# First chunk of the down product: operand sums by adding DMA transfers, half of the gated values stored negated

## The chip, the cores and the metric

The kernel runs on one core of a Trainium2 chip. PE is the matrix engine, PEld its weight loads, DVE the vector engine, ACT the scalar engine, POOL the GpSimd engine, SP the engine that only issues DMAs. Each engine carries out its instructions in order; they meet through semaphores. The metric is device time in microseconds (us), the median of several runs of one kernel.

## What is computed

One decoder block over 512 tokens of 2048 channels in float32: a combined input projection that feeds two token mixers, an output projection, and a gated MLP with a causal convolution of width 3 between its up projection and its activation. The change lies in the MLP:

```python
h = _rmsnorm(x, norm2_g[l])
up = jnp.einsum('bsd,df->bsf', h, ffn_w_up[l])          # 2048 -> 2 * 6144
up = _causal_dwconv(up, ffn_conv_w[l], ffn_conv_b[l])
gate, val = jnp.split(up, 2, axis=-1)
x = x + jnp.einsum('bsf,fd->bsd', jax.nn.gelu(gate) * val, ffn_w_down[l])
...
return _rmsnorm(x, final_g)
```

## The kernel before

**Seven products in place of eight.** Both MLP products treat every operand as 2 x 2 blocks of 256 columns and use seven block products on sums and differences of the blocks (a Winograd form of Strassen's scheme). Each operand therefore is a tile of seven slots: the blocks themselves (slots 4 to 6, and 7 for making sums) and sums of them (slots 0 to 3). Every operand is also split into a high part in a rounded format (ACT, L126) and the rest (DVE, L127), and each product is three matmuls over these halves; a pair of such tiles is what PE reads.

**Units.** The work runs in units of one weight operand each: 192 for the up product (24 blocks of eight, blocks alternating between gate and value columns), then the down product in three chunks of 8, 8 and 6 operands, four blocks for each. A unit is 42 matmuls of 256 columns (`product`, L852), seven products of six; their order is 1, 2, 6, 5, 3, 7, 4. Unit 184 begins the last up block, unit 192 the first down block. Products gather in eight PSUM banks, seven for a block and one to spare, so the second product of a block takes over a bank of the block before. The banks are read at a block's end: in the up product by `combine` (ACT copies product 1, L868; DVE L869 to L876), in the down product by L969 to L979.

**The stream.** `stream` lists the operands in the order in which they are wanted: weights (`Weights`) for each unit, and, in the units 187 to 197, the activations of the down product's first chunk (`Acts`, eight operands, numbered 0 to 7 here; after units 187, 188, 190, 191, 193, 194, 196 and 197). `prepare` walks it and puts, for item n, the load of n+1, the sums of n+1, the split of n and the load of n+2 into the program. Loads go to SP's queue into one of three buffers `q`. The weights of most units load their four blocks (512 KB, L637) and DVE makes the sums (L646 to L648). Those of units 0 to 7 and of the units around each chunk's start (184 to 199 for the first) load prepared sums from memory instead (512 KB, L639) and three blocks (384 KB, L640). A unit's preparation is written ahead of its own matmuls, and reaches two units ahead.

**Sums prepared in memory.** POOL's queue issues DMA transfers that copy and add into DRAM tiles `made`; `make` (L315 to L322) takes the next ones from a list, a share of it in every unit of the up product. A transfer that adds to a tile waits on POOL for the one before it on that tile, and the list lays the four stages of a tile apart.

**The gated values.** In an up block of value columns, DVE finishes the convolution (L916), multiplies by the gate (L919), and POOL issues the store of the 512 columns into the DRAM tile `ad` (L921), 256 KB, two blocks of 256. This and the other steps of a block's tail are put off by `later` into units 1, 2, 4 and 5 of the block that follows. For the down product, `Acts.load` brings an `ad` tile back (L665) and `Acts.sums` makes its sums with three DVE instructions (L671 to L673):

```python
nc.vector.tensor_tensor(q[:, 2:4], q[:, 7:8].broadcast_to([P, 2, 256]), q[:, 5:7], ALU.subtract)
nc.vector.tensor_tensor(q[:, 1], q[:, 6], q[:, 2], ALU.subtract)
nc.vector.tensor_tensor(q[:, 0], q[:, 4], q[:, 1], ALU.subtract)
```

Of the kernel before, what the change touches and what calls it, by code (L numbers as in the profile page):

```python
# [8 lines left out]
F32 = mybir.dt.float32  # L9
# [3 lines left out]
ALU = mybir.AluOpType  # L13

P = 128
# [31 lines left out]
CHUNKS = [range(0, 8), range(8, 16), range(16, 22)]  # L47
# [31 lines left out]
def hybrid_block(ctx: ExitStack, tc: tile.TileContext, x, xT, w_in, w_out, w_up, w_dn, w_m4, w_dl, wab, wsT, vec, bs, vgb, fg, out):  # L79
    nc = tc.nc  # L80
# [213 lines left out]
    made = {}  # L294
# [13 lines left out]
    to_make = []  # L308
# [3 lines left out]
                to_make += copies[n] if part == 0 else added[n][0] if part == 1 else [added[n][1][part - 2]]  # L312
    pace = const.tile([P, 1], F32, name="pace")

    def make(n, after=None):  # L315

        if after is not None:
            nc.gpsimd.tensor_copy(pace, after)
        for _ in range(min(n, len(to_make))):
            add, dst, src = to_make.pop(0)  # L320
            how = {"accum_op": ALU.add} if add else {}
            nc.gpsimd.dma_start(dst, src, max_dma_last_dim=8192, **how)  # L322

# [192 lines left out]
    for i in range(2):  # L516
        for st in range(NS):
            t = vv[i][:, st]
# [5 lines left out]
    for i in range(2):  # L524
        ps = project(w_in, B_U + i, xg, True)
        t = rp.tile([P, 4, S], F32, name="uu", tag="r")
# [77 lines left out]
    ss2 = const.tile([P, NS, 4], F32, name="ss2")  # L604
    x2d = [tc.dram_tile([P, NS, 512], F32, name=f"x2d{d}") for d in range(4)]
    ad = [tc.dram_tile([P, 4, 256], F32, name=f"ad{i}") for i in range(NP)]

    def squares2(d):
        nc.gpsimd.dma_start(x2d[d], x2[d])
# [18 lines left out]
    class Weights:  # L628


        def __init__(self, src, made=None):
            self.src, self.made = src, made
# [9 lines left out]
        def sums(self):  # L642
            q = self.q
            if self.made is not None:
                return
            nc.vector.tensor_tensor(q[:, 2:4], q[:, 5:7], q[:, 7:8].broadcast_to([P, 2, 256]), ALU.add)  # L646
            nc.vector.tensor_tensor(q[:, 1], q[:, 2], q[:, 6], ALU.add)  # L647
            nc.vector.tensor_tensor(q[:, 0], q[:, 1], q[:, 4], ALU.add)  # L648
# [7 lines left out]
    class Acts:  # L656


        def __init__(self, m, src=None, fill=None):
            self.m, self.src, self.fill = m, src, fill  # L660

        def load(self):
            self.q = slots("q")
            if self.fill is None:
                nc.sync.dma_start(self.q[:, 4:8], self.src)  # L665
            else:
                self.fill(self.q)

        def sums(self):
            q = self.q  # L670
            nc.vector.tensor_tensor(q[:, 2:4], q[:, 7:8].broadcast_to([P, 2, 256]), q[:, 5:7], ALU.subtract)  # L671
            nc.vector.tensor_tensor(q[:, 1], q[:, 6], q[:, 2], ALU.subtract)
            nc.vector.tensor_tensor(q[:, 0], q[:, 4], q[:, 1], ALU.subtract)  # L673
# [33 lines left out]
    def rest_of_loads():  # L707
        while halves:
            halves.pop(0)()
# [54 lines left out]
    spread = (0, 1, 3, 4, 6, 7, 9, 10)  # L764
    after = {}
    for m in range(8):
        after.setdefault(max(2, m), []).append(Acts(m, fill=from_rows(m)))
    for c, s in zip(CHUNKS, starts):
        for i, p in enumerate(c):
            after.setdefault(s - 8 + spread[i] + 3, []).append(Acts(i, src=ad[p]))  # L770

    def half_tiles(d):
        if d < 3:
# [82 lines left out]
    def later(step, f):  # L856
        lazy.setdefault(step, []).append(f)
# [22 lines left out]
    def up_block(g, val, u0):  # L880
        q = {}
        for m in range(8):
            prepare(ready(u0 + m))
            for p in ORDER:
                product(q, p, act[m], stream[place[u0 + m]].hl, True, m == 0, m == 7)
                if p == 6:
                    rest_of_loads()
            make(len(to_make) - n_make + n_make * (u0 + m + 1) // (n_up - 16))
            if m == 7 and u0 == 0:
                pads[:] = [t_tile(f"pad{n}", [P, 2, S + 2]) for n in range(2)]  # L890
                for t in pads:
                    nc.gpsimd.memset(t[:, :, 0:2], 0.0)
            for f in lazy.pop(u0 + m, ()):
                f()
        c1 = t_tile("c1", [P, 2, 256])
        lo, hi = slice(2, 258), slice(258, 514)
        combine(q, c1, pads[0][:, :, lo], pads[1][:, :, lo], pads[0][:, :, hi], pads[1][:, :, hi])
        if u0 == 0:
            pools["ps"].release()
            pools["tr"].release()  # L900
            pools["ps"] = psum("q1", 8)

        def tap(n, j, f):
            if val:
                dst = t_tile("cv", [P, 2, S])if j == 0 else cvs[n]
                cvs[n] = dst
            else:
                if j == 0:
                    gates[n] = t_tile("gate", [P, 2, S], 2)
                dst = gates[n]  # L910
            nc.scalar.activation(dst[:, j], pads[n][:, j, 2:2 + S], AF.Identity, bias=col(V_FB + f), scale=col(V_FW + 2 * 96 + f))

        def rest(n, j, f):
            dst = (cvs if val else gates)[n][:, j]
            for i in (1, 0):
                nc.vector.scalar_tensor_tensor(dst, pads[n][:, j, i:i + S], col(V_FW + i * 96 + f), dst, ALU.mult, ALU.add)  # L916
            if val:
                gate = gates[n][:, j]
                nc.vector.tensor_tensor(gate, gate, dst, ALU.mult)  # L919
                at = 0 if j else 2  # L920
                nc.gpsimd.dma_start(ad[2 * g + n][:, at:at + 2], gate.rearrange("p (a b) -> p a b", a=2))  # L921

        def gelu(n, j):
            t = gates[n][:, j]
            nc.scalar.activation(t, t, AF.Gelu_apprx_tanh)

        cvs = {}
        at = u0 + 8
        for i, (n, j) in enumerate(((1, 0), (1, 1), (0, 0), (0, 1))):
            f = 48 * val + 4 * g + 2 * n + j  # L930
            step = at + (0, 1, 3, 4)[i]
            later(step, lambda n=n, j=j, f=f: tap(n, j, f))
            later(step + 1, lambda n=n, j=j, f=f: rest(n, j, f))
            if not val:
                later(step + 2, lambda n=n, j=j: gelu(n, j))

    pads = []
    for b, (g, val) in enumerate(ups):
# [6 lines left out]
    def down_block(ci, n, u0):  # L945
        tt = nc.vector.tensor_tensor
        size = len(CHUNKS[ci])
        q = {}
        for m in range(size):
            prepare(ready(u0 + m))  # L950
            if m == (6 if u0 == n_up else 1):
                if u0 == n_up:

                    pools["t"].release()
                    pools["x"] = pool("tx", "right")

            for half, at in ((0, 6 if u0 == n_up else 1), (1, 6 if u0 == n_up else 3)):
                if m == at:
                    t = pools["x"].tile([P, 2, 512], F32, name="xs", tag="xs", bufs=3)
                    nc.gpsimd.dma_start(t, x2d[n][:, 2 * half:2 * half + 2])  # L960
                    xs[n, half] = t
            for p in ORDER:
                product(q, p, act[m], stream[place[u0 + m]].hl, False, m == 0, m == size - 1)
            for f in lazy.pop(u0 + m, ()):
                f()
        X1, X2 = xs[n, 0], xs[n, 1]
        X11, X12, X21, X22 = X1[:, :, 0:256], X1[:, :, 256:512], X2[:, :, 0:256], X2[:, :, 256:512]
        c6, c5, c7 = (pools["x"].tile([P, 2, 256], F32, name="cc", tag="cc", bufs=3) for _ in range(3))
        tt(X11, X11, q[1], ALU.add)  # L969
        tt(X11, X11, q[2], ALU.add)  # L970
        nc.scalar.copy(c6, q[6])
        tt(c6, c6, q[1], ALU.subtract)
        nc.scalar.copy(c5, q[5])
        tt(X12, X12, q[3], ALU.add)
        nc.scalar.copy(c7, q[7])
        tt(X21, X21, q[4], ALU.add)
        steps = [
            lambda: tt(c5, c5, c6, ALU.add),
            lambda: tt(X12, X12, c5, ALU.add),  # L979
            lambda: tt(c6, c6, c7, ALU.add),  # L980
            lambda: tt(X21, X21, c6, ALU.subtract),
            lambda: tt(c5, c5, c7, ALU.add),
            lambda: tt(X22, X22, c5, ALU.add),
        ]
        if u0 + size == len(units):
            prepare(len(stream) - 2)
            for f in steps:
                f()
            prepare(len(stream) - 1)
            return  # L990
        at = u0 + size
        for i in range(3):
            later(at + i, steps[2 * i])
            later(at + i, steps[2 * i + 1])
        for half, t, step in ((0, X1, 0), (1, X2, 2)):
            later(at + step, lambda half=half, t=t: nc.gpsimd.dma_start(x2d[n][:, 2 * half:2 * half + 2], t))
# [6 lines left out]
    for n in DORD[:3]:  # L1003
        t = slots("q").rearrange("p a b -> p (a b)").rearrange("p (a b) -> p a b", a=NS)
# [9 lines left out]
    for st in range(NS):  # L1014
# [4 lines left out]
        for n, (i, d, lo, hi) in enumerate(pieces):  # L1019
# [6 lines left out]
            t = xs[d, st // 2][:, st % 2, lo:hi]  # L1026
# [10 lines left out]
        v, y, u, r = (const.tile([P, 1], F32, name=f"r3{c}", tag=f"r3{c}", bufs=2) for c in "vyur")  # L1037
# [7 lines left out]
        for n in order:  # L1045
            _, d, lo, hi = pieces[n]
# [74 lines left out]
```

## Time and profile before

| | |
|---|---|
| median of 3 runs | 2078.45 us (2078.12 to 2079.34) |
| the profiled execution | 2073.06 us, its span 2071.3 us |
| granted TensorE clock over the span | 0.995 |
| loads `q<-ad` of the down product's chunks | 22, 512 KB each, 3.1 to 7.8 us from issue to landing |
| transfers into `made` | 270 of 256 KB and 54 of 128 KB |
| stores `ad<-gate` | 48 of 256 KB |

Rows of a timeline give the start in us from the span's start, the duration, the engine, the line of the kernel, the operation, the tiles it writes and reads, and in brackets how long the engine sat idle before it and what released it. Rows of waits give who waited for whom, the total in us, how often, and the longest. Rows of groups give busy us, the mean of one in ns, and the idle time before. Rows of DMA issues give the queue that issued, how many, the size of each and the median us from issue to landing. Rows of stretches give the busy us of PE, PEld, DVE, ACT and POOL with their counts, the granted clock, the share of the 16 DMA engines' time, and GB/s. In names of tiles, `wh` and `wl` are the high and low halves of a weight, `ah` and `al` those of an activation, `qs` a PSUM bank, `q` a loaded operand.

### The profile page before, as it was taken

To read this page: it belongs to the slowest core of one execution; us is meant where nothing else is said; L and a number is where in the kernel's file an instruction comes from. 1 tells how busy PE (TensorE), PEld (TensorE's weight loads), DVE (VectorE), ACT (ScalarE), POOL (GpSimd) and SP (SyncE) were. 2 spreads that over 40 slices of the span, in tenths; PEclk is the share of its full clock that TensorE was granted. 3 is DMA by queue.
4 is the path that set the end of the run, shared out by engine and by line. 5 is a ranking of instruction groups with operands and counts; after the bars stand their busy time and mean duration, and the time that the engine had idled before them with its cause. 6 is when DMAs were issued, how large, how long until landed. Compare 5 with 4: busy or idle time off the path is not lost.

```text
span 2071.3 us, 35056 instructions
## 1 busy us (share of the span) xinstructions
PE 2037.6 (98%) x14528; PEld 1921.8 (93%) x14528; DVE 1732.0 (84%) x2183; ACT 906.6 (44%) x887; POOL 323.7 (16%) x510
## 2 busy tenths in 40 slices
PE   9999999999989999999999999999999999999998
PEld 8888888888789999999999999999999999999996
DVE  7598982745379999999999999999989979879986
ACT  6445322423274444444444444444455345345443
POOL 1332232211210202202202012022000000000001
PEclk9999999999999999999999999999999999999999
DMA  7666687656553746647557467466456568558564
GB/s 250 181 171 163 175 213 175 192 170 213 148 156 112 199 127 177 180 131 193 148 151 203 136 173 191 136 175 168 128 205 221 189 216 284 181 192 282 176 231 153
DMA packets 105904, 376.37 MB, mean 182 GB/s; under 512 B 14608, under 2 KB 22160, under 8 KB 91792
## 3 DMA queue, kind: packets, MB, share of 16 engines
q1 hardware_dynamic: 65808, 246.30, 35.1%
q0 software_dynamic: 39360, 127.17, 25.9%
q8 instruction: 113, 1.85, 0.4%
q10 hardware_dynamic: 576, 0.66, 0.1%
q14 instruction: 47, 0.39, 0.1%
HBM read 341.57 MB, written 110.36 MB: 218 GB/s over the span
## 4 chain that ended last, share of the span: by engine, by line
PE 76%; DVE 17%; DMA 4%; issue 2%; ACT 1%; DVEq 0%; SPq 0%; ACTq 0%
PE qs L852 46%; PE ps L162 9%; PE ps L164 9%; PE ps L163 9%; DVE wl L127 7%; DMA q<-w_up 3%; DVE q L646 2%; DVE al L127 1%; DVE q L647 1%; DVE cv L916 1%; DMA q<-w_dn 1%; PE qs L163 1%; PE qs L162 1%; PE qs L164 1%; DVE gate L916 1%
## 5 line engine op out<-in xcount | busy, mean ns | idle before, releaser
L852 PE MATMUL qs<-ah,wh 128*128 128x256 f32 x2688 | 765.1, 285 | 6.4 <-DVE pad L869 3.9
L852 PE MATMUL qs<-al,wh 128*128 128x256 f32 x2688 | 762.5, 284 | 0.0
L852 PE MATMUL qs<-ah,wl 128*128 128x256 f32 x2688 | 762.3, 284 | 0.0
L126 ACT CAST wh<-q 128x1792 fp32r<-128x1792 f32 (+1 forms) x282 | 476.8, 1691 | 597.5 <-PE qs L852 382.9
L127 DVE TENSOR_TENSOR wl<-q,wh 128x1792 fp32r<-128x1792 f32 (+1 forms) x282 | 567.7, 2013 | 43.6 <-ACT wh L126 43.3
L852 PEld LDWEIGHTS qs<-ah,wh 128*128 128x128 f32 x2688 | 517.3, 192 | 9.3 <-DVE pad L869 5.1
L852 PEld LDWEIGHTS qs<-al,wh 128*128 128x128 f32 x2688 | 517.3, 192 | 0.1
L852 PEld LDWEIGHTS qs<-ah,wl 128*128 128x128 f32 x2688 | 517.3, 192 | 0.0
L852 PE MATMUL qs<-wh,ah 128*128 128x256 f32 x1232 | 351.0, 285 | 7.0 <-ACT c L868 3.4
L852 PE MATMUL qs<-wl,ah 128*128 128x256 f32 x1232 | 350.2, 284 | 0.0
L852 PE MATMUL qs<-wh,al 128*128 128x256 f32 x1232 | 350.1, 284 | 0.0
L852 PEld LDWEIGHTS qs<-wh,ah 128*128 128x128 f32 x1232 | 237.8, 193 | 8.5 <-ACT c L868 3.6
L322 POOL DMA_DIRECT2D made<-w_m x324 | 234.9, 1061 | 54.0 <-DMA made<-w_m 44.8
L127 DVE TENSOR_TENSOR wl<-wraw,wh 128x1024 fp32r<-128x1024 f32 (+2 forms) x105 | 118.0, 1127 | 149.4 <-ACT wh L126 144.5
L852 PEld LDWEIGHTS qs<-wl,ah 128*128 128x128 f32 x1232 | 237.9, 193 | 0.2 <-DVE wl L127 0.2
L852 PEld LDWEIGHTS qs<-wh,al 128*128 128x128 f32 x1232 | 237.8, 193 | 0.0
L126 ACT CAST wh<-wraw 128x1024 fp32r<-128x1024 f32 (+2 forms) x105 | 102.1, 974 | 273.4 <-PE ps L163 146.4
L646 DVE TENSOR_TENSOR q<-q 128x512 f32<-128x512 f32 x226 | 154.8, 685 | 22.1 <-DMA q<-w_up 18.6
L921 POOL DMA_DIRECT2D ad<-gate x48 | 28.0, 583 | 828.3 <-DVE gate L919 828.3
L162 PE MATMUL ps<-xgh,wh 128*128 128x512 f32 x384 | 152.5, 398 | 0.0
L163 PE MATMUL ps<-xgl,wh 128*128 128x512 f32 x384 | 152.2, 397 | 0.0
L164 PE MATMUL ps<-xgh,wl 128*128 128x512 f32 x384 | 150.2, 396 | 0.0
(242 smaller groups left out, 2491.5 us busy)
## 6 DMA issues: line engine op xcount, KB each, us to landing
q<-w_up SPq DMA_DIRECT2D x176, 512.0 KB, 3.6
made<-w_m POOLq DMA_DIRECT2D x270, 256.0 KB, 5.9
wraw<-w_in SPq DMA_DIRECT2D x28, 1024.0 KB, 6.3
q<-made SPq DMA_DIRECT2D x54, 512.0 KB, 4.0
q<-w_dn SPq DMA_DIRECT2D x50, 512.0 KB, 3.8
wraw<-w_out SPq DMA_DIRECT2D x16, 1024.0 KB, 5.5
q<-w_dn SPq DMA_DIRECT2D x38, 384.0 KB, 4.6
ad<-gate POOLq DMA_DIRECT2D x48, 256.0 KB, 2.4
```

The source lines that it names most:

```text
L126: nc.scalar.copy(h, src)
L127: nc.vector.tensor_tensor(l, src, h.bitcast(F32), ALU.subtract)
L162: nc.tensor.matmul(ps, lhsT=ah, rhs=bh, start=start, stop=False)
L163: nc.tensor.matmul(ps, lhsT=ah, rhs=bl, start=False, stop=False)
L164: nc.tensor.matmul(ps, lhsT=al, rhs=bh, start=False, stop=stop)
L322: nc.gpsimd.dma_start(dst, src, max_dma_last_dim=8192, **how)
L646: nc.vector.tensor_tensor(q[:, 2:4], q[:, 5:7], q[:, 7:8].broadcast_to([P, 2, 256]), ALU.add)
L647: nc.vector.tensor_tensor(q[:, 1], q[:, 2], q[:, 6], ALU.add)
L852: nc.tensor.matmul(q[p][:, t], lhsT=x_, rhs=y_, start=first and t == 0 and n == 0, stop=last and t == 1 and n == 2, skip_group_check=True)
L916: nc.vector.scalar_tensor_tensor(dst, pads[n][:, j, i:i + S], col(V_FW + i * 96 + f), dst, ALU.mult, ALU.add)
L921: nc.gpsimd.dma_start(ad[2 * g + n][:, at:at + 2], gate.rearrange("p (a b) -> p a b", a=2))
```

## The change

For the eight operands of the first chunk, the sums are made in memory. Transfers on POOL's queue copy blocks of `ad` into a new DRAM tile `sums_of` and add further blocks to it, five transfers for each operand, one with every second unit from the 81st unit on. [...] `Acts.load` then brings the prepared sums (512 KB) and three blocks (384 KB), and `Acts.sums` does nothing for these operands. Where the down product's first chunk reads products that came out negated, additions become subtractions. The other two chunks stay as they were.

```diff
-    def make(n, after=None):
+    def make(n, after=None, todo=to_make):
...
-        for _ in range(min(n, len(to_make))):
-            add, dst, src = to_make.pop(0)
+        for _ in range(min(n, len(todo))):
+            add, dst, src = todo.pop(0)
...
+    sums_of = [tc.dram_tile([P, 4, 256], F32, name=f"as{i}") for i in CHUNKS[0]]
...
         def load(self):
             self.q = slots("q")
-            if self.fill is None:
+            if self.made is not None:
+                nc.sync.dma_start(self.q[:, 0:4], self.made)
+                nc.sync.dma_start(self.q[:, 4:7], self.src[:, 0:3])
+            elif self.fill is None:
                 nc.sync.dma_start(self.q[:, 4:8], self.src)
...
         def sums(self):
+            if self.made is not None:
+                return
...
+            if u0 >= 80 and m % 2:
+                make(1, todo=sum_up)
             make(len(to_make) - n_make + n_make * (u0 + m + 1) // (n_up - 16))
...
-                nc.vector.tensor_tensor(gate, gate, dst, ALU.mult)
+                if 2 * g + n in CHUNKS[0]:
+                    for t in (slice(0, 256), slice(256, 512)):
+                        nc.vector.scalar_tensor_tensor(gate[:, t], gate[:, t], -1.0 if (t.start == 0) == (j == 1) else 1.0, dst[:, t], ALU.mult, ALU.mult)
+                else:
+                    nc.vector.tensor_tensor(gate, gate, dst, ALU.mult)
...
+    sum_up = []
+    for k in range(len(CHUNKS[0]) + 3):
+        for r in range(4):
+            if 0 <= k - r < len(CHUNKS[0]):
+                dst, src = sums_of[k - r], ad[k - r]
+                sum_up += [
+                    [(0, dst[:, 0:2], src[:, 0:3:2]), (0, dst[:, 2:4], src[:, 1:3])],
+                    [(1, dst, src[:, 3:4].broadcast_to([P, 4, 256]))],
+                    [(1, dst[:, 0:2], src[:, 1:2].broadcast_to([P, 2, 256]))],
+                    [(1, dst[:, 0], src[:, 2])],
+                ][r]
...
+        plus = ALU.subtract if ci == 0 else ALU.add
...
-        tt(X11, X11, q[2], ALU.add)
+        tt(X11, X11, q[2], plus)
...
-        tt(X12, X12, q[3], ALU.add)
+        tt(X12, X12, q[3], plus)
...
-            lambda: tt(c5, c5, c6, ALU.add),
+            lambda: tt(c5, c6, c5, plus),
...
-            lambda: tt(c6, c6, c7, ALU.add),
+            lambda: tt(c6, c6, c7, plus),
...
-            lambda: tt(c5, c5, c7, ALU.add),
+            lambda: tt(c5, c5, c7, plus),
```

More of the change, by code (lines that the diff above doesn't have):

```diff
@@ L656, in hybrid_block, with __init__ @@
     class Acts:
-        def __init__(self, m, src=None, fill=None):
-            self.m, self.src, self.fill = m, src, fill
+        def __init__(self, m, src=None, fill=None, made=None):
+            self.m, self.src, self.fill, self.made = m, src, fill, made
         def load(self):
             self.q = slots("q")
-            if self.fill is None:
+            if self.made is not None:
+                nc.sync.dma_start(self.q[:, 0:4], self.made)
+                nc.sync.dma_start(self.q[:, 4:7], self.src[:, 0:3])
+            elif self.fill is None:
                 nc.sync.dma_start(self.q[:, 4:8], self.src)
@@ L769, in hybrid_block @@
         for i, p in enumerate(c):
-            after.setdefault(s - 8 + spread[i] + 3, []).append(Acts(i, src=ad[p]))
+            after.setdefault(s - 8 + spread[i] + 3, []).append(Acts(i, src=ad[p], made=sums_of[i] if c is CHUNKS[0] else None))
     def half_tiles(d):
```

## The prediction

> **What bounds the kernel now.** I read the page first, then the waits of PE, then three stretches of the trace. The page says that PE is busy nearly throughout, so only the places where it falls behind can be won:
>
> ```profile
> span 2071.3 us, 35056 instructions
> PE 2037.6 (98%) x14528; PEld 1921.8 (93%) x14528; DVE 1732.0 (84%) x2183; ACT 906.6 (44%) x887; POOL 323.7 (16%) x510
> ```
>
> The sums that the change takes off DVE stand at 1528 to 1594 us. In ten-microsecond stretches (busy time of PE, PEld, DVE, ACT, POOL; granted clock; DMA share) only two of that time are bad for PE, and the PE timeline shows the place, the first unit of the down product (unit 192):
>
> ```profile
> 1560.00:1570.00 10.00, 6.32 (x45) 5.82 (x44) 9.15 (x10) 6.13 (x6) 0.00 (x0) 0.85 0.69 243
> 1570.00:1580.00 10.00, 9.66 (x67) 9.66 (x68) 9.47 (x12) 3.98 (x4) 0.00 (x0) 0.80 0.41 143
> ...
> 1564.39 0.28 PE L852 MATMUL qs<-wh,al 128*128 128x256 f32 x1
> 1568.07 0.58 PE L852 MATMUL qs<-wh,ah 128*128 128x256 f32 x1 [3.40 <-ACT c L868]
> ...
> 1570.34 0.58 PE L852 MATMUL qs<-wh,ah 128*128 128x256 f32 x1 [0.62 <-DVE pad L869]
> ...
> 1574.05 0.28 PE L852 MATMUL qs<-wh,al 128*128 128x256 f32 x1
> 1574.17 0.28 PE L852 MATMUL qs<-wh,ah 128*128 128x256 f32 x1
> ```
>
> From 1564.39 to 1574.05 PE starts 24 matmuls (products 2, 6, 5 and 3 of the unit, six each). At the 0.12 us between the last two rows they need 2.9 us; they took 9.66. **This junction costs 6.8 us**: 3.4 and 0.6 of idle, the rest matmuls at a low clock. What was late, on ACT and DVE, with the load behind it on SP's queue:
>
> ```profile
> 1565.85 1.69 ACT L126 CAST ah<-q 128x1792 fp32r<-128x1792 f32 x1 [1.44 <-DVE q L673]
> 1567.44 0.58 ACT L868 COPY c<-qs 128x512 f32<-128x512 f32 x1
> ...
> 1560.10 0.32 SPq L665 DMA_DIRECT2D q<-ad  x1
> ...
> 1564.21 0.69 DVE L671 TENSOR_TENSOR q<-q 128x512 f32<-128x512 f32 x1 [0.75 <-DMA q<-ad]
> ...
> 1565.73 2.02 DVE L127 TENSOR_TENSOR wl<-q,wh 128x1792 fp32r<-128x1792 f32 x1
> 1567.67 2.02 DVE L127 TENSOR_TENSOR al<-q,ah 128x1792 fp32r<-128x1792 f32 x1
> 1569.60 0.68 DVE L869 TENSOR_TENSOR pad<-c,qs 128x512 f32<-128x512 f32 x1
> 1570.20 0.69 DVE L871 TENSOR_TENSOR v<-qs,c 128x512 f32<-128x512 f32 x1
> ```
>
> The copy L868 frees the bank that PE's second product wants. It stands on ACT behind the cast of operand 4 of the chunk, that cast behind the three sums L671 to L673, and these behind a load that took 4.1 us (1560.10 to 1564.2). So the sums stand in the chain that PE waits for, once.
>
> The change also touches the up product, 682 to 1497 us: the stretch itself, DVE's waits, PE's waits and DVE's groups there.
>
> ```profile
> 682.00:1496.70 814.70, 810.36 (x6726) 807.82 (x6726) 774.12 (x981) 366.51 (x300) 141.71 (x202) 1.00 0.59 165
> ...
> DVE q L646 <- DMA q<-w_up: 18.6, 19, 2.5
> ...
> PE qs L852 <- DVE pad L869: 2.1, 3, 1.4
> PE qs L852 <- DVE v L875: 2.1, 7, 0.3
> ...
> L646 DVE TENSOR_TENSOR q<-q 128x512 f32<-128x512 f32 x161 | 110.3, 685 | 18.6 <-DMA q<-w_up 18.6
> L647 DVE TENSOR_TENSOR q<-q 128x256 f32<-128x256 f32 x160 | 68.0, 425 | 5.5
> L916 DVE SCALAR_TENSOR_TENSOR cv<-pad,vc,cv 128x512 f32<-128x512 f32 x80 | 59.9, 749 | 1.4
> L919 DVE TENSOR_TENSOR gate<-gate,cv 128x512 f32<-128x512 f32 x40 | 27.7, 692 | 1.4
> ```
>
> DVE works 774.1 us, waits 18.6 for loads and never for PE or ACT; the remaining 22 us are gaps of hundredths between its instructions. PE waits only for DVE, at the ends of blocks. **So DVE sets the pace of the up product**, and work or load waits added to it there lengthen the kernel about one for one.
>
> **The change part by part.**
>
> *A. The junction.* Five of the eight sum triples (operands 0 to 4) go from in front of L868, each 1.52 us start to start (1564.21 to 1565.73). But each operand then loads 512 + 384 KB, not 512, and it has only three buffers: a load starts when the subtraction L127 of the item three places earlier ends. The loads of this stretch, 1500 to 1620 us, medians from issue to landing, and one slow one:
>
> ```profile
> q<-made SPq DMA_DIRECT2D x16, 512.0 KB, 3.7
> q<-ad SPq DMA_DIRECT2D x8, 512.0 KB, 3.4
> ...
> q<-w_dn SPq DMA_DIRECT2D x8, 384.0 KB, 4.2
> ...
> 1541.23 0.32 SPq L665 DMA_DIRECT2D q<-ad  x1
> ...
> 1547.55 0.69 DVE L671 TENSOR_TENSOR q<-q 128x512 f32<-128x512 f32 x1 [2.96 <-DMA q<-ad]
> 1549.08 2.02 DVE L127 TENSOR_TENSOR wl<-q,wh 128x1792 fp32r<-128x1792 f32 x1
> ```
>
> A pair of 512 and 384 KB, what a weight with prepared sums loads, lands 0.4 + 4.2 = 4.6 us after the first issue; the slow load took 6.3. The chain to L868 is then: the subtraction of unit 190's weights ends (now 1551.1; it started at 1549.08 because the sums before it waited for the slow load), operand 3 loads, cast 1.7, subtraction 2.0, operand 4 loads, cast 1.7, L868. Without the sums ahead of it, that first subtraction ends at 1548 to 1550. With 1548.5 and loads of 5.2 (between 4.6 and 6.3, nearer to 4.6, since these bytes are added where the DMA share is 0.4 to 0.7), L868 comes at 1548.5 + 2 x 5.2 + 5.4 = 1564.3, which PE, wanting it at 1564.5, does not notice. L869 follows operand 4's subtraction and ends at 1564.3 + 2.0 + 0.6 = 1566.9; PE's third product wants its bank at 1563.8 + 1.4 = 1565.2. So 1.7 us of idle stay, and **A = -5.1 us**. Ends: loads of 4.6 behind 1547.7 give L868 at 1562.3 and no stall (-6.8); loads of 6.3 behind 1550.1 give 1568.1 and no gain (0).
>
> The low clock matters for what stays. An idle of 1.40 us left the clock alone, the one of 3.40 us halved it:
>
> ```profile
> 955.77 0.39 PE L852 MATMUL qs<-ah,wh 128*128 128x256 f32 x1 [1.40 <-DVE pad L869]
> 954.00:956.00 2.00, 0.60 (x6) 0.40 (x5) 2.00 (x3) 1.04 (x1) 1.95 (x3) 1.00 0.94 191
> ...
> 1568.00:1570.00 2.00, 1.65 (x6) 1.36 (x6) 2.00 (x2) 1.61 (x2) 0.00 (x0) 0.50 0.52 178
> ```
>
> I take 1.7 us as the first kind. The Trainium skill, "TensorE: Matmul & The Clock Gate", Part 1, says the same: half rate comes after an idle window of about 3.4 us. Were the clock lost after any idle, A would be about 2.5 us smaller; these rows speak for the rule.
>
> *B. The end of that block.* DVE is late once more, 1610 to 1620 us:
>
> ```profile
> PE qs L852 <- DVE xs L970: 1.1, 1, 1.1
> PE qs L852 <- ACT cc L971: 0.5, 1, 0.5
> ```
>
> Operands 5 to 7 take another 4.6 us off DVE, which starts L869 3.3 us earlier too: 7.9 against PE's 5.1. **B = -1.0** (0 to -1.6).
>
> *C. The sign.* In 16 places of the up product one multiply of 512 columns (692 ns) becomes two scaled ones of 256. 256 columns fewer save 685 - 425 = 260 ns, so a scaled one of 256 takes 749 - 260 = 490 ns. Independent instructions overlap by 0.08 (L869 lasts 0.68, L871 starts 0.60 later), so 2 x 0.41 - 0.61 = 0.21 each. **C = +3.3 us**, on the engine that sets the pace (2.1 if 0.13 each; 4.6 without overlap).
>
> *D. The adding transfers.* 40 issues on POOL's queue from unit 81 to 159: per operand 2 x 256 KB copied and 512 + 256 + 128 KB added, 1408 KB, 11.5 MB for eight. POOL runs ahead between gated stores, so they come in bursts with the other adding transfers. The load of one unit in a burst, 1029 to 1050 us, and outside, 1055 to 1090, and the stretch's transfers into the prepared weights:
>
> ```profile
> q<-w_up SPq DMA_DIRECT2D x4, 512.0 KB, 7.7
> ...
> q<-w_up SPq DMA_DIRECT2D x8, 512.0 KB, 3.5
> ...
> made<-w_m POOLq DMA_DIRECT2D x133, 256.0 KB, 8.2
> made<-w_m POOLq DMA_DIRECT2D x29, 128.0 KB, 7.2
> ```
>
> DVE's 18.6 us of load waits go with 162 such transfers, 0.115 us each; 40 more give 4.6. Against that, the new ones move rows of 1 to 2 KB, those of now mostly 8 KB by the code, and a load that shares the engines in turn waits for less. I take **D = +3.0** (0, as no transfer leaves the stretch, to 10, twice the cost by bytes). POOL has time (141.7 of 814.7 us busy); behind a new wait on its queue stand only gated stores and weights needed much later. The loads themselves are issued on SP, which has no new order.
>
> Turned signs in the down product are the same number of DVE instructions of the same shapes, so nothing; were they slower, the later junctions would show it.
>
> The sum: -5.1 - 1.0 + 3.3 + 3.0 = **+0.2 us**. The profiled execution took 2073.06 (span 2071.3), 5.4 below the median shown; I put the difference on the median: 2078.45 + 0.2 = 2078.6, say **2078.6 us**, no change.
>
> **The rivals.**
>
> *The transfers are hidden* (faster). If rows of 1 to 2 KB leave room for the loads, D is 0, and with the junctions cleared whole the sum is -6.8 - 1.6 + 3.3 = -5.1, **2073.4**. For it: a load delayed by 4.2 us in a burst has half its way shared with 8 KB rows. The Trainium skill, "DMA: Bandwidth & Descriptors", Queues, rings and completion order, has each DMA engine take queues in turn, packet by packet, which points this way; no row here shows 1 KB adds alone. Chance 0.28.
>
> *The bursts grow into DVE's path* (slower). Each burst already fills the DMA engines for some 20 us; five of them get eight transfers more per 81 us. If adding small rows is slow, loads stay at 7.7 us for twice as long and D is 9: -6.1 + 3.3 + 9 = +6.2, **2084.7**. It decides from D above 7. Chance 0.20.
>
> *The junction stays* because the larger loads land as late as the sums did: A about -1, B 0: +5.3, **2083.8**. It decides when a load pair takes over 6 us. Chance 0.08. That the sums stay on DVE can't be: the method returns at once.
>
> **How the numbers follow.** Forecast 0.44, rivals 0.28, 0.20 and 0.08. A measurement of this kernel tells about 0.2%, 4.2 us, from no change: faster 0.28, same 0.44, slower 0.28. The forecast's own range is 2074.5 to 2082.5; to hold 8 in 10 with both rivals' middles it is 2072.5 to 2085.5.
>
> **What would show it.** Right: no L671 to L673 for this chunk; L868 near 1564 + C + D and PE idle there under 2 us at full clock; DVE busy some 3 us more before 950 us; DVE's waits for the up loads 18.6 + 3 after it. Wrong: a wait for L868 over 3 us with operand loads above 6 us (A), up load waits above 25 us or below 19 (D), or PE waits in the up product that don't grow with DVE's work (C).

## The result: slower, and the profile after

| | before | changed |
|---|---|---|
| median | 2078.28 us (4 runs, 2074.13 to 2079.34) | 2097.78 us (4 runs, 2095.60 to 2102.37) |
| ratio to before | 1 | 1.0105, 95% interval 1.0091 to 1.0118 |
| span of the profiled execution | 2071.3 us | 2094.5 us |

The forecast was 2078.6 us, no change, with a range to 2085.5. The time lies above the range; the outcome is the rival in which the bursts grow into DVE's path, and larger than its 2084.7. The spans differ by 23.2 us, the medians by 19.5: the profiled execution of before lies 5.4 us under its median, so differences of the two traces come out some 4 us larger than those of the medians.

The head of the changed kernel's page, and PE's waits for DVE:

```profile
span 2094.5 us, 35107 instructions
PE 2043.8 (98%) x14528; PEld 1925.2 (92%) x14528; DVE 1722.1 (82%) x2175; ACT 907.4 (43%) x887; POOL 360.0 (17%) x550
...
PE qs L858 <- DVE pad L875: 19.2, 13, 4.7
...
PE qs L858 <- DVE wl L127: 4.0, 3, 2.2
PE qs L858 <- DVE v L881: 3.7, 13, 0.3
PE qs L858 <- DVE xs L998: 2.7, 2, 1.5
```

DVE works 10 us less than before (1722.1 against 1732.0) and the kernel takes 23 us more: what PE waits for is still DVE, and DVE is late for a reason other than its work. The wait for the copy of product 1 (L874 now) is gone from the list.

**Where the time went.** The gated stores are marks that both traces share. POOL's timeline, before, at the store for unit 81 (ahead of which one new transfer was issued in the changed kernel) and at the same store in the last up block:

```profile
1008.42 0.60 POOL L921 DMA_DIRECT2D ad<-gate  x1 [47.05 <-DVE gate L919]
...
1496.73 0.60 POOL L921 DMA_DIRECT2D ad<-gate  x1 [39.19 <-DVE gate L919]
```

The same two stores in the changed kernel:

```profile
1013.20 0.61 POOL L934 DMA_DIRECT2D ad<-gate  x1 [47.14 <-DVE gate L932]
...
1526.74 0.60 POOL L934 DMA_DIRECT2D ad<-gate  x1 [39.15 <-DVE gate L932]
```

The changed kernel is 4.8 us behind at the first, 30.0 at the second, and 23.2 at the end of the span. So **25.2 us are lost in the stretch with the adding transfers, and 6.8 us are won after it**. DVE's waits for the up loads, the changed kernel from 682 to 1013 and from 1013 to 1527 us:

```profile
DVE q L647 <- DMA q<-w_up: 11.7, 10, 2.4
...
DVE q L647 <- DMA q<-w_up: 35.8, 17, 4.7
```

Before, the waits of the whole stretch were 18.6, and those of the second part are:

```profile
DVE q L646 <- DMA q<-w_up: 10.6, 11, 2.5
```

The second part grew from 10.6 to 35.8, by 25.2 us, the loss of that stretch. None of these waits is longer than 4.7 us; there are 17 instead of 11, and longer ones. The 4.8 us of the first part are 3.7 of load waits (8.0 before, 11.7 here) and 1.1 of the signs. Only the first of the 40 transfers is issued in that part, and in the runs below that keep every transfer as it was there, the same waits come to between 8.3 and 11.8: sums of waits scatter by some 4 us from trace to trace, and the 25.2 holds no closer than that.

A burst shows how. Busy time of the engines, clock and DMA share, before, in the stretches after the same store:

```profile
1029.00:1050.00 21.00, 21.00 (x177) 21.00 (x176) 19.01 (x25) 9.31 (x8) 9.81 (x14) 1.00 1.00 252
1050.00:1070.00 20.00, 20.00 (x169) 20.00 (x168) 17.70 (x22) 9.59 (x9) 0.00 (x0) 1.00 0.36 104
```

And in the changed kernel:

```profile
1029.00:1050.00 21.00, 20.69 (x171) 20.44 (x171) 20.28 (x28) 8.79 (x7) 11.60 (x17) 1.00 0.97 234
1050.00:1070.00 20.00, 20.00 (x169) 20.00 (x168) 14.20 (x18) 8.57 (x8) 4.79 (x5) 1.00 1.01 255
1070.00:1090.00 20.00, 17.47 (x132) 17.06 (x132) 19.38 (x26) 8.53 (x8) 0.00 (x0) 0.91 0.33 107
```

The DMA engines stay full for another 20 us (the store before these stretches lies 4.8 us later here). In these DVE works 14.2 us of 20, not 17.7. PE pays 20 us later, when it reaches the end of the block and DVE is not there: 17.47 of 20 us busy and the clock down to 0.91. So the place of the transfers shows almost no idle time of PE; it stands here:

```profile
1084.89 0.58 PE L858 MATMUL qs<-ah,wh 128*128 128x256 f32 x1 [2.33 <-DVE pad L875]
```

**The junction** at unit 192 did what the change was made for. ACT and DVE of the changed kernel:

```profile
1590.90 1.69 ACT L126 CAST ah<-q 128x1792 fp32r<-128x1792 f32 x1 [1.04 <-DMA q<-ad]
1592.50 0.58 ACT L874 COPY c<-qs 128x512 f32<-128x512 f32 x1
...
1589.90 2.02 DVE L127 TENSOR_TENSOR wl<-q,wh 128x1792 fp32r<-128x1792 f32 x1 [1.31 <-ACT wh L126]
1592.62 2.02 DVE L127 TENSOR_TENSOR al<-q,ah 128x1792 fp32r<-128x1792 f32 x1 [0.70 <-ACT ah L126]
1594.57 0.68 DVE L875 TENSOR_TENSOR pad<-c,qs 128x512 f32<-128x512 f32 x1
```

The cast now waits for its load alone. PE's longer wait there (another, of 0.3 us, follows at 1598.8), and the clock over the ten microseconds:

```profile
1595.30 0.39 PE L858 MATMUL qs<-wh,ah 128*128 128x256 f32 x1 [0.61 <-DVE pad L875]
1590.00:1600.00 10.00, 9.07 (x74) 8.70 (x73) 8.99 (x10) 6.58 (x6) 0.00 (x0) 1.00 0.76 269
```

Unit 192 takes 6.5 us from its first matmul to the first of the next unit (1593.09 to 1599.56), where it took 11.8 (1563.79 to 1575.60): 5.3 us less. At 0.12 us each its 42 matmuls need 5.0, so it costs 1.4 us, not 6.8. The wait at the end of that block has not shrunk: it was 1.1 and 0.5 us, and is now

```profile
PE qs L858 <- DVE xs L998: 1.5, 1, 1.5
```

### The profile page after: what moved, and what is told of

Its sections match the earlier page's. It is cut to its first block, busy times and chain, and to the rows that moved or that the text cites. A ratio compares the mean times of both kernels' runs of the same rounds, so it can differ in the third digit from the quotient of the medians.

```text
span 2094.5 us, 35107 instructions
## 1 busy us (share of the span) xinstructions
PE 2043.8 (98%) x14528; PEld 1925.2 (92%) x14528; DVE 1722.1 (82%) x2175; ACT 907.4 (43%) x887; POOL 360.0 (17%) x550
## 4 chain that ended last, share of the span: by engine, by line
PE 69%; DVE 19%; DMA 8%; issue 2%; ACT 2%; SPq 0%; DVEq 0%; ACTq 0%
PE qs L858 41%; PE ps L164 9%; PE ps L162 9%; PE ps L163 9%; DVE wl L127 8%; DMA q<-w_up 6%; DVE q L647 2%; DVE q L648 1%; DVE cv L924 1%; DMA q<-w_dn 1%; DVE al L127 1%; DMA q<-ad 1%; PE qs L163 1%; PE qs L164 1%; PE qs L162 1%
## 5 line engine op out<-in xcount | busy, mean ns | idle before, releaser
L858 PE MATMUL qs<-ah,wh 128*128 128x256 f32 x2688 | 768.0, 286 | 22.0 <-DVE pad L875 18.6
L322 POOL DMA_DIRECT2D made<-w_m x324 | 249.5, 1073 | 63.7 <-DMA made<-w_m 38.8
```

What stands on the lines that cost most here:

```text
L858: nc.tensor.matmul(q[p][:, t], lhsT=x_, rhs=y_, start=first and t == 0 and n == 0, stop=last and t == 1 and n == 2, skip_group_check=True)
```

## The experiments

Theory after the result: *transfers*, the adding transfers keep the DMA engines busy and DVE waits longer for the loads of the up product. Rival: *sign*, the scaled multiplies cost more than their length. Ratios are to the kernel before, run beside it on the same chip; differences in us are of the medians, where nothing else is said.

**The sign alone.** Two multiplies of 256 columns with a factor of 1 or -1, in place of one of 512, store half of the gated values of these operands negated. No transfers; DVE makes the sums, with additions:

```diff
-            if u0 >= 80 and m % 2:
-                make(1, todo=sum_up)
...
+            if self.plus:
+                nc.vector.tensor_tensor(q[:, 2:4], q[:, 7:8].broadcast_to([P, 2, 256]), q[:, 5:7], ALU.add)
+                nc.vector.tensor_tensor(q[:, 1], q[:, 6], q[:, 2], ALU.add)
+                nc.vector.tensor_tensor(q[:, 0], q[:, 4], q[:, 1], ALU.add)
+                return
```

> Half of the gated values are stored negated and DVE makes the operands' sums with additions; no adding transfers, no larger loads. Theory 'transfers' (the added time is DVE waiting for the up loads while the adding transfers fill the DMA engines): within 5 us of before, 1 to 4 us slower, DVE's waits for up loads between 682 and 1500 us at 18 to 23 us, as before, the junction at unit 192 still standing with a wait for the copy of product 1 over 3 us. Rival 'sign' (the two scaled multiplies on the engine that sets the pace cost more than their length): 10 us slower or more.

Measured: 2080.08 us, ratio 1.0013 (1.0000 to 1.0025). The rival falls. DVE's waits for the loads are 23.4 us, just above the 23 that was expected at most; the wait for the copy stands, but at 1.8 us, not over 3:

```profile
PE qs L857 <- ACT c L873: 1.8, 1, 1.8
```

This wait scatters: it is 1.8 to 2.5 us in the six runs here that keep the order at the junction and DVE's sums, and the 3.4 of before is the longest. What unit 192 costs them, reckoned as above, is 5.4 to 7.0 us. One place in DVE's timeline shows the length, the two scaled multiplies together and what follows them:

```profile
697.00 0.76 DVE L927 SCALAR_TENSOR_TENSOR gate<-gate,cv 128x256 f32<-128x256 f32 x2
697.68 0.68 DVE L646 TENSOR_TENSOR q<-q 128x512 f32<-128x512 f32 x1
698.40 0.42 DVE L647 TENSOR_TENSOR q<-q 128x256 f32<-128x256 f32 x1
698.86 0.42 DVE L648 TENSOR_TENSOR q<-q 128x256 f32<-128x256 f32 x1
699.20 2.02 DVE L127 TENSOR_TENSOR wl<-q,wh 128x1792 fp32r<-128x1792 f32 x1
701.14 1.53 DVE L921 SCALAR_TENSOR_TENSOR cv<-pad,vc,cv 128x512 f32<-128x512 f32 x2
```

The pair takes 0.68 us from start to start against the 0.61 that I reckoned for one multiply: 0.07 in each of 16 places, 1.1 us. One scaled multiply lasts 422 ns on average (L927 from 682 to 1013 us, 12.2 us for 32).

**The transfers alone.** The kernel before with the 40 transfers, which nothing reads:

```diff
+            if u0 >= 80 and m % 2:
+                make(1, todo=sum_up)
```

> The kernel before plus the 40 transfers into memory that nothing reads. Theory 'transfers': 20 to 30 us slower than before (the 25 us by which DVE's load waits grew, and the junction's stall of 6.8 us stays), with DVE's waits for the up loads 40 us or more instead of 18.6. Rival 'sign': within 6 us of before.

Measured: 2107.33 us, ratio 1.0148 (1.0120 to 1.0177). DVE's waits, 1013 to 1500 us:

```profile
DVE q L647 <- DMA q<-w_up: 41.3, 17, 6.1
```

The transfers alone cost 29 us, which covers all that the change costs (19.5) and what the loads alone win (5.0, next).

**The loads alone.** The sums of the first chunk are left out; the operands load 512 + 384 KB, the stored values in the place of the sums.

```diff
-            after.setdefault(s - 8 + spread[i] + 3, []).append(Acts(i, src=ad[p]))
+            after.setdefault(s - 8 + spread[i] + 3, []).append(Acts(i, src=ad[p], made=ad[p] if c is CHUNKS[0] else None))
```

> The first chunk's operands load 512 + 384 KB and DVE makes no sums for them; the sums are left out (what is loaded in their place is the stored values), no transfers, no signs. If the junction is cleared as in the changed kernel: 6 to 8 us faster than before, PE without a wait for the copy of product 1 and at full clock there. If the larger loads take the gain back: within 2 us.

Measured: 2073.28 us, ratio 0.9976 (0.9963 to 0.9989), 5.0 us faster, a little less than expected. PE's waits there, 1540 to 1660 us:

```profile
PE qs L857 <- DVE xs L975: 1.4, 1, 1.4
PE qs L857 <- DVE pad L874: 0.7, 1, 0.7
PE qs L857 <- DVE v L880: 0.3, 1, 0.3
```

There is no wait for the copy, and the larger loads do not take the gain back. Unit 192 costs 1.5 us here, 3.9 to 5.5 less than in the runs with the sums on DVE, which agrees with the time.

**Rows of 8 KB, and copies in place of adds.** Two runs ask what in a transfer is dear. The first moves the same bytes in the same number of transfers, in long rows; the second keeps the short rows and adds nothing. Nothing reads what they write.

```diff
+                dst, src = (t.rearrange("(a b) c d -> a (b c d)", b=2) for t in (sums_of[k - r], ad[k - r]))
+                sum_up += [
+                    [(0, dst[0:32], src[0:32]), (0, dst[32:64], src[32:64])],
+                    [(1, dst, src)],
+                    [(1, dst[0:32], src[32:64])],
+                    [(1, dst[0:16], src[32:48])],
+                ][r]
```

> As the run with the transfers alone, with the same number of transfers, the same bytes, copies and adds, but in rows of 8 KB instead of 1 and 2 KB (the values are no sums; nothing reads them). Theory 'rows' (small rows make them dear): 10 us slower than before or less, a half of the other's cost or less. Theory 'bytes' (the bursts grow with the bytes): within 5 us of the run with small rows, 18 to 30 us slower than before.

> As the run with the transfers alone, all 40 of them plain copies of the same shapes, none adding. Theory 'bursts' (DVE loses time for as long as the engines stay full past the first 20 us): a copy moves its bytes once where an add also reads what it adds to, so the bursts are shorter; 10 to 22 us slower than before. Rival 'adds are free' (only the small rows count): within 3 us of the run with the adds, about 29 us slower.

Measured: long rows 2099.92 us, ratio 1.0115 (1.0090 to 1.0141); copies 2102.15 us, ratio 1.0112 (1.0097 to 1.0128). Long rows come out between the two expectations, 22 us slower: in the range of 'bytes' against before, but 7 us from the run with small rows. Copies are 24 us slower, above the 10 to 22 of 'bursts' and below the rival's 29. POOL's queue, its packets, MB and share of the engines' time from 1013 to 1500 us, with short rows, in the run with the transfers alone:

```profile
q0 software_dynamic: 18688, 40.64, 42.0%
```

With long rows:

```profile
q0 software_dynamic: 11936, 40.64, 37.1%
```

With copies:

```profile
q0 software_dynamic: 13312, 40.64, 36.4%
```

The same 40.64 MB take 5 points less of 487 us in either. DVE's waits with long rows, in the same stretch, against 41.3 with short ones:

```profile
DVE q L647 <- DMA q<-w_up: 29.3, 17, 4.8
```

By the medians, long rows save some 7 of the 29 us and copies some 5, but both intervals (up to 1.0141 and 1.0128) overlap that of the short rows with adds (from 1.0120), so that neither saving is shown for certain; some 22 us stay with both kinds. Short rows do not spare the loads.

**Half the density.** The changed kernel, transfers on every fourth unit from unit 25.

```diff
-            if u0 >= 80 and m % 2:
+            if u0 >= 24 and m % 4 == 1:
```

> The changed kernel with its 40 transfers on every fourth unit from unit 25 on, so that a burst gets four of them instead of eight, over twice as many bursts. Theory 'bursts' (the first us of a longer burst are sheltered, the later ones are not): less than half of the 25 us stays, 2 us faster to 8 us slower than the kernel before. Rival 'a price for each' (each transfer costs the same wherever it stands): as the changed kernel, 18 us or more slower than before.

Measured: 2100.00 us, ratio 1.0104 (1.0089 to 1.0119), the changed kernel's time. My expectation missed; the rival's is met. DVE's waits from 682 to 1500 us:

```profile
DVE q L647 <- DMA q<-w_up: 46.2, 23, 5.9
```

That is 27.6 more than before, 0.7 for each transfer, in bursts half as much enlarged: four transfers more in a burst are no cheaper, each, than eight.

**Forty fewer.** The other side: 40 of the adds into the prepared weights are left out, so that these sums lack a part.

```diff
+            if 80 <= u0 < 160 and m % 2:
+                to_make.pop(next(i for i, t in enumerate(to_make) if t[0]))
```

> The kernel before with 40 of the adds into the prepared weights left out, one with every second unit from 81 to 159 (their sums are incomplete, so the output isn't the reference's). It asks what a transfer of a burst costs below the level of before. Theory 'kink' (the first 20 us of a burst lie where DVE does not need the loads, what is beyond costs 0.6 us for each transfer): DVE's load waits between 1013 and 1500 us fall from 10.6 only to 5 to 8 us, that is by some 0.1 us for each. Rival 'a price for each': they fall to 0 to 2 us.

Measured: 2074.76 us, ratio 0.9978 (0.9967 to 0.9989). The waits, 1013 to 1500 us:

```profile
DVE q L646 <- DMA q<-w_up: 3.3, 4, 1.0
```

They fall from 10.6 to 3.3, 0.18 us for each. That is less than 'kink' expected to stay and more than 'a price for each' did; neither is met, and the scatter of some 4 us reaches both. Forty more of the change's kind cost 25.2 / 40 = 0.63 each, in long rows (29.3 - 10.6) / 40 = 0.47. Of the 10.6 us that there were, forty could not have saved more than 0.27 each. So the price rises with the load: some 0.2 below the level of before, and two to three times that above it.

**Holding the transfers back.** POOL copies one element (of each partition) of the low half of the unit's weights, which DVE writes, before it issues, so that it cannot run ahead:

```diff
-                make(1, todo=sum_up)
+                make(1, stream[place[u0 + m]].hl[1][:, 0, 0:1].bitcast(F32), todo=sum_up)
```

in the changed kernel, for the new transfers only, and in the kernel before for those of the weights:

```diff
-            make(len(to_make) - n_make + n_make * (u0 + m + 1) // (n_up - 16))
+            make(len(to_make) - n_make + n_make * (u0 + m + 1) // (n_up - 16), stream[place[u0 + m]].hl[1][:, 0, 0:1].bitcast(F32))
```

> The changed kernel, with each of the 40 transfers held on POOL until DVE has split the weights of its unit, so that they and the transfers behind them come one by one and not in a burst. Theory 'bursts': most of the 25 us goes, 0 to 8 us faster than the kernel before the change, DVE's load waits between 682 and 1530 us at 25 us or less. Rival 'work' (the DMA engines simply have that much more to do): within 6 us of the changed kernel, about 20 us slower than before.

> The kernel before, with the adding transfers of the weights held back in the same way, unit by unit, nothing else changed. Theory 'bursts': DVE's 18.6 us of load waits go down, to 10 or less, and the time by 4 to 10 us. Rival 'work': within 3 us of before.

Measured: the changed kernel 2086.47 us, ratio 1.0038 (1.0023 to 1.0053); the kernel before 2069.13 us, ratio 0.9954 (0.9938 to 0.9971). **Without its bursts the kernel before is 9 us faster.** DVE's waits there, 682 to 1500 us:

```profile
DVE wl L127 <- ACT wh L126: 10.3, 10, 1.2
DVE q L646 <- DMA q<-w_up: 4.3, 3, 1.7
```

And the issues of the up loads where the burst stood, 1029 to 1070 us, with the size and the median time to landing:

```profile
q<-w_up SPq DMA_DIRECT2D x9, 512.0 KB, 3.6
```

Waits and time of this kernel are as the theory expected. The loads land in 3.6 us again, 18.6 us of waits become 4.3, and now DVE waits for ACT; PE is busy 816.2 of the 818 us and sets the pace. The changed kernel got back 11 of its 19.5 us. It lies 8.4 us above before, between the two expectations, and meets neither; only every second unit holds POOL here, so that two units' transfers still come together. Its waits are still above the 18.6 of before:

```profile
DVE q L647 <- DMA q<-w_up: 31.6, 18, 5.0
```

**All of them held back**, the new ones as in the change or on every fourth unit:

> The same with the 40 transfers where the change has them, on every second unit from unit 81 on, one behind the unit's own. Theory 'bursts': as the run with half the density or a few us slower, 8 to 16 us faster than before. Rival 'work': 0 to 8 us slower than before, as with the new transfers alone held back.

> The changed kernel with all of POOL's transfers in the up product held back unit by unit, and the 40 new ones on every fourth unit from unit 25 on. Theory 'bursts': nearly all of the cost goes, DVE's load waits between 682 and 1500 us at 10 us or less, and the junction's gain adds to the one of the kernel before when paced: 12 to 18 us faster than before. Rival 'work' (the engines have too much to do in any order): load waits above 20 us, and slower than the paced kernel before.

Measured: 2074.75 us, ratio 0.9980 (0.9971 to 0.9988), and 2075.05 us, ratio 0.9981 (0.9971 to 0.9991). Both beat the kernel before, by some 4 us, and by the ratios lose to it when it is paced too (0.9954, its interval ending at 0.9971, where these begin). Neither expectation of either run is met: 'bursts' wanted 8 us or more, 'work' a slower kernel than before, or in the second run waits above 20 us. DVE's waits from 682 to 1500 us, as in the change:

```profile
DVE q L647 <- DMA q<-w_up: 19.2, 13, 4.0
```

On every fourth unit:

```profile
DVE q L647 <- DMA q<-w_up: 15.6, 11, 3.0
```

Against the 4.3 of the paced kernel before, the 40 transfers cost 0.37 and 0.28 us each. Against 0.63 in the bursts, some half of the price goes with the bursts, as the theory says, and some half stays, as the rival 'work' says. Why it stays is argued, not shown: a load has little slack. In the timeline above, between the end of one subtraction, when a load into its buffer is issued, and the sums that need it lie the next sums and subtraction, 697.68 to 701.14, 3.46 us. Where a convolution stands between, it is more; a unit takes 814.7 / 160 = 5.1 us on average. Outside a burst the load takes 3.5. A fourth buffer would test it directly; that was not tried.

**The junction without transfers.** The paced kernel before, with operands 4 and 5 one unit later:

```diff
-    spread = (0, 1, 3, 4, 6, 7, 9, 10)
+    spread = (0, 1, 3, 4, 7, 8, 9, 10)
```

> The kernel before with POOL's transfers held back unit by unit, and the down product's operands 4 and 5 of a chunk prepared one unit later, so that the cast of operand 4 no longer stands on ACT ahead of the copy of product 1 at unit 192; no other transfers, no signs. If the junction's stall is an order on ACT, the wait for that copy goes and the time is 3 to 6 us under the paced kernel, 12 to 15 us under before. If only less work for DVE clears it, the stall comes back as a wait for DVE and the time is within 2 us of the paced kernel's, 9 us under before.

Measured: 2069.82 us against 2081.22 for before beside it, ratio 0.9946 (0.9932 to 0.9959), not to be told from the paced kernel's 0.9954; 11 us under before lies between the two expectations. PE's waits, 1540 to 1640 us, and two of them in its timeline:

```profile
PE qs L852 <- DVE wl L127: 3.1, 2, 2.3
PE qs L852 <- DVE xs L970: 1.4, 1, 1.4
PE qs L852 <- DVE pad L869: 0.7, 1, 0.7
PE qs L852 <- DVE v L875: 0.3, 1, 0.3
...
1559.86 0.39 PE L852 MATMUL qs<-wh,ah 128*128 128x256 f32 x1 [0.75 <-DVE pad L869]
...
1582.04 0.38 PE L852 MATMUL qs<-wl,ah 128*128 128x256 f32 x1 [2.27 <-DVE wl L127]
```

The wait for the copy is gone, and unit 192 itself is cleared: it waits 0.75 and 0.3 us at full clock, as in the changed kernel, where the paced kernel waits 2.5 for the copy and 1.3 more. But a wait for the weights' subtraction has come 22 us later, after which the clock is 0.50 (1584 to 1586 us); an operand's sums (1578.45 to 1579.97) stand on DVE in front of that subtraction. So in the paced kernel the order on ACT was what held unit 192, and the new order moves the stall instead of removing it. The loads alone, where DVE has less to do, cleared the junction without such a wait and won 5.0 us.

## Why the prediction was wrong

- **A, the junction: right.** The chain was the one described: with the sums gone, L868 is in time, and 0.6 and 0.3 us of idle stay at full clock, not 1.7. Unit 192 became 5.3 us shorter, where 5.1 was forecast, and the loads alone won 5.0.
- **B, the end of that block: wrong.** 1.0 us forecast, nothing measured: 1.6 us of waits before, 1.5 after. The forecast counted only the work taken off DVE. In the changed kernel DVE waits 4.3 us for ACT's casts from 1594 to 1640 us, where it waited 0.4 before (1569 to 1616), and ACT waits there 13.7 us for loads, where it waited 5.7 before. That the larger loads were what held the casts fits these waits; no run tests it alone. That the two traces give -6.8 after the transfers (30.0 to 23.2), close to the -6.1 of A and B together, is in part luck: 1.4 us of it lie ahead of unit 192 and behind the block, where nothing was forecast.
- **The clock.** The prediction took an idle of 1.7 us to leave the clock alone, and that was never put to the test at the junction. But half rate came here after shorter idles than the window of about 3.4 us that the Trainium skill, "TensorE: Matmul & The Clock Gate", Part 1, names for it. At 1084.89 above, 2.33 us halved it; so did 2.33 us at unit 192 in the run with 8 KB rows (first line below, clock 0.50 from 1591 to 1593) and 1.84 us in the run with the sign alone (0.50 from 1575 to 1576). With forty fewer, 2.19 us left it at 1.00, and 1.29 us soon after brought it down (the other two lines; 0.50 from 1569 to 1570). So the length of one idle did not decide it.

```profile
1590.62 0.58 PE L853 MATMUL qs<-wh,ah 128*128 128x256 f32 x1 [2.33 <-ACT c L869]
...
1566.82 0.39 PE L852 MATMUL qs<-wh,ah 128*128 128x256 f32 x1 [2.19 <-ACT c L868]
1569.09 0.58 PE L852 MATMUL qs<-wh,ah 128*128 128x256 f32 x1 [1.29 <-DVE pad L869]
```

- **C, the sign: right mechanism, too large.** 3.3 forecast, 1.1 by length. The overlap of 0.08 us was right (0.42 us long, 0.34 from start to start); the length was not: 422 ns for a scaled multiply of 256 columns, where 490 had been worked out from the longer ones. In time the sign alone is 1.8 us by the medians, within the noise of the load waits.
- **D, the adding transfers: the step that failed.** 3.0 forecast; 25.2 measured in the traces, and 29 by the medians in the run with the transfers alone, beyond its upper end of 10. Its mechanism, DVE waiting for loads that share the engines, was right; its size was not. Two choices made it. "DVE's 18.6 us of load waits go with 162 such transfers, 0.115 us each" took an average for the price of one more, when the price of the next 40 was 0.63. And I went below even that because rows of 1 to 2 KB would leave the loads room; the run with 8 KB rows shows long ones no dearer (1.0115 against 1.0148), and DVE's waits shorter with them (29.3 against 41.3). The turn-taking that the Trainium skill, "DMA: Bandwidth & Descriptors", Queues, rings and completion order, describes packet by packet did not make short rows kind to the loads in any run here.
- The row that spoke against it stood in the prediction: 7.7 us from issue to landing in a burst. Beside the 3.46 us that DVE leaves a load at the least, and the 5.1 of an average unit, it says that a load in a longer burst is late by some 2.6 to 4.2 us. The 25.2 us are 5.0 for each of five bursts, the lateness of one or two such loads. The low DMA share after a burst (0.36 above) is no room for the new transfers as long as POOL runs ahead: they lengthen the burst.
- That DVE sets the pace of the up product one for one: right for waits that are added, and the reason why the error in D went into the time whole. It does not hold for waits that are taken away: in the paced kernel 14.3 us of them went, the time fell by 9, and PE set the pace.

## What to carry to other kernels

Price added traffic by the slack of the loads beside it, latency in a busy stretch against the time between a buffer's release and its next use, and not by the average wait of the traffic that is there. When the bounding engine waits for loads, look first at when a queue that runs ahead releases its transfers: here one small copy as a brake was worth 9 us, more than the 6.8 that the whole change was aimed at. And a saving on the last stall of a chain must be set against the cost in every block before it.

## What had not been expected of the hardware

From 1013 to 1500 us, the transfers of POOL's queue with adds in 1 and 2 KB rows took 42.0% of the engines' time, with 8 KB rows 37.1%, and with copies 36.4%, for the same 40.64 MB. The kernels with them lost 29, 22 and 24 us; with intervals that overlap, whether the time follows the share is not shown. An idle of PE well under the 3.4 us of the prediction's row halved its clock: 2.33 us in two runs, 1.84 in a third, while 2.19 in a fourth did not.
